# A hybrid encoder layer on one core: a tile of its own for half of the second projection tile's weights, other early orders, two projection blocks more ahead of the first scores, and a scaled copy moved into mask columns

## The chip, the cores and the metric

The kernel runs on one core of a Trainium2 chip. A core has a matrix engine (PE, with its weight loads shown as PEld), a vector engine (DVE), a scalar engine (ACT), a general engine (POOL) and a sync engine (SP) that issues most transfers. Each takes its instructions in a fixed order and they meet at semaphores. The metric is device time of one execution in microseconds, from runs of the whole program; the median of three counts.

## The reference

One encoder layer on 1024 tokens of width 1024, in float32. An RMS norm feeds one projection into 2304 columns, which serve two token mixers side by side.

```python
hn = rmsnorm(h, norm_mix[l])
proj = jnp.einsum('bsd,de->bse', hn, w_in[l])
qa, ka, va, qb, kb, vb = jnp.split(proj, splits, axis=-1)
...
o_a = window_gqa_sink(qa, ka, va, sink[l])
o_b = neighbourhood_attention(...)
mix = jnp.concatenate([rmsnorm(o_a, norm_a[l]), rmsnorm(o_b, norm_b[l])], axis=-1)
h = h + jnp.einsum('bse,ed->bsd', mix, w_out[l])
hn = rmsnorm(h, norm_ffn[l])
h = h + conv_gated_mlp(hn, w_gate[l], w_up[l], conv_w[l], conv_b[l], w_down[l])
return rmsnorm(h, norm_final)
```

Group A is attention in a window of 128 tokens either side, with 8 query heads on 2 key heads, rotated first quarters of the heads, and a sink logit in each softmax. Group B has 8 heads on a 16 by 64 grid of tokens with windows of 8 by 16 and a bias by relative position. Then come the output projection, a gated MLP of width 2816 with a convolution of three taps on the gate, and a last norm.

## The kernel before, in words

**Layout.** Activations stand transposed, features on the 128 partitions and 1024 tokens along the free axis. Nearly every product is made of two-part numbers: a value is split into a high part (written by ACT, which rounds it) and a low part (the remainder, by DVE or POOL), and a product is three matmuls, high by high, low by high, high by low. One such triple on 128 by 512 is a *block* (lines 172 to 174, in the loop of `product` line 180). A projection tile of 128 output columns takes 16 blocks: 2 halves of the tokens by 8 tiles of the inner axis k.

**The head of the program.** The first two projection tiles run together while x arrives (lines 742 to 747): for each k the scaled x tile is split (`split_scaled`, lines 191 and 192, high part on ACT, low part on DVE), and PE makes four blocks, two token halves by two tiles, into the PSUM banks `pj` and `o`. The weights of k = 0 to 3 of both come into four tiles that are made at the start; those of k = 4 to 7 go through `load_w`, that is a transfer into `raw` (2 buffers, line 150), the high part on ACT into `whi` (3 buffers, line 156) and the low part into `wlo` (3 buffers, line 157). Tiles of one name rotate: with three buffers, the fourth tile waits until the first one's readers are done. Beside this ACT squares the x tiles (line 211) and DVE adds the squares (line 213), for the norm.

**The third projection tile** (`third`, lines 750 to 757, 16 blocks into the bank `s`) fills PE while the norm is made. One of its blocks comes first; then 8 transposes of the summed squares (line 784); five blocks; 8 transposes that spread the inverse root over the partitions (line 266, called at 791); then the ten left. Between the two sets of transposes DVE sums (lines 785, 786) and POOL raises to the power of minus a half (line 787). The result `rstd` scales every evacuation of a projection from PSUM (`evacuate`, line 272).

**From a projection to attention.** `rotate` (lines 288 to 294) sends 16 rows of each head away by transfers, turns them on DVE and brings them back; the queries are then split and stacked (`split_first` lines 313 and 314 for the first query tile, `split_pair` lines 301 to 306 for others, `split_first_k` and `split_k` for keys).

**Attention.** There are 48 units: 16 window units (8 query blocks for each of 2 key heads, 4 heads each) and 32 grid units (8 heads by 4 pairs of query blocks). A softmax step (`softmax`, lines 465 to 495) starts with a score on PE (line 439), takes bias and row minimum on DVE (line 469) into a buffer of the rotation `p` (6 buffers), the exponential on ACT (line 473), the reciprocal on DVE (line 474), and then goes one of several ways. On way T, POOL scales (line 477) and PE transposes (line 501), and ACT and DVE split the transposed tile (lines 504, 505). On way D and Q the high part is made on ACT (line 488); the low part on D is one DVE pass (line 490), and on Q two POOL passes: a scaled copy `y` (line 493), which takes another buffer of the same rotation `p`, and the difference (line 494). Then a transposing transfer on SP (line 495) brings the result to `turned`, from where PE multiplies with the values (lines 528 and 604), and ACT and DVE take the sums out of PSUM (lines 539 and 543, 618 and 620). All 64 grid softmaxes are on way Q or T, 48 of them on Q.

**What sets the order.** PE's order is the program's own: it is written down as it stands. Between the steps of attention a generator, `rest()`, hands out blocks of the remaining projections (tiles 3 to 17, then the part of the output projection that needs group A alone); `fill(n)` takes n of them. `FILL0` blocks run before the first score, and `RATES` says how many are spread over each stretch of 8 window units or 4 grid units. The other engines' order is made by a scheduler which places an instruction when its model finds it ready, by priority; `behind(names)` keeps an instruction after a marked one. The weights of a later tile are fetched and split by `load` (k = 0 to 3) and `load_rest` (k = 4 to 7) of `Project`.

The constants tile `cst` holds the identity, the window mask (`K_MA`, 384 columns), the grid mask (`K_MB`) and a column of scales. Once attention is over, small vectors of the MLP's scales are taken from the window mask's columns (`littles`, line 1015).

## Time and profile before

| what | value |
| --- | --- |
| median of three runs | 1028.16 us (1027.82 to 1031.29) |
| profiled execution, its own time | 1027.81 us |
| its span, first to last instruction | 1026.0 us |
| PE busy | 1009.7 us, 98% |
| DVE, ACT, POOL busy | 875.6, 676.3, 216.4 us |
| granted PE clock, mean | 0.997 |

Busy time is the union of an engine's instructions. The rows of the timeline give start, duration, engine, line, operation, output and inputs, shape and count, and in brackets the engine's idle time before the row with what ended it. Matmuls are pipelined, so a matmul row lasts longer than the distance to the next one's start; what a wait costs PE is read from starts.

### The profile page before, as it was taken

What the parts mean: (1) busy time and instruction counts of PE and PEld (TensorE: products, weight loads), DVE (VectorE), ACT (ScalarE), POOL (GpSimd) and SP (SyncE); (2) the same over time, 40 slices, a digit from 0 to 9 for tenths busy, and PEclk for the clock granted to TensorE, in tenths of its full rate; (3) what the DMA queues carried; (4) which work ended last, traced back from release to release, by engine and by line L of the source; (5) the groups of instructions that cost most, each with busy time, mean ns of one, the idle gap of its engine ahead of it and who ended that gap; (6) DMA issues with size and microseconds to landing.
All of it is one profiled execution on the core that took longest, in us unless ns stands there. A gap on an engine that the chain in (4) does not pass through costs nothing.

```text
span 1026.0 us, 15565 instructions
## 1 busy us (share of the span) xinstructions
PE 1009.7 (98%) x5102; PEld 577.8 (56%) x5102; DVE 875.6 (85%) x1714; ACT 676.3 (66%) x1242; POOL 216.4 (21%) x339
## 2 busy tenths in 40 slices
PE   9999999999999999999999999999999999999997
PEld 7877777777775545544444444444444444444446
DVE  6799988767898899999897988788888888999875
ACT  8667787768687687645777777754634666655551
POOL 2235455877866210001000000000000000000002
PEclk9999999999999999999999999999999999999998
DMA  8556564787799875201787767633232788978744
GB/s 314 198 133 139 115 138 106 159 155 137 136 195 216 280 255 171 82 1 42 251 279 251 266 230 256 232 114 134 82 114 103 256 263 291 309 245 269 250 147 165
DMA packets 143938, 191.79 MB, mean 187 GB/s; under 512 B 77360, under 2 KB 88112, under 8 KB 143856
## 3 DMA queue, kind: packets, MB, share of 16 engines
q1 hardware_dynamic: 133264, 164.84, 55.9%
q10 hardware_dynamic: 10592, 25.95, 6.6%
q8 instruction: 40, 0.66, 0.3%
q14 instruction: 42, 0.34, 0.1%
HBM read 132.81 MB, written 28.57 MB: 157 GB/s over the span
## 4 chain that ended last, share of the span: by engine, by line
PE 65%; DVE 2%; DMA 1%; ACT 1%; issue 0%; POOL 0%; DVEq 0%; ACTq 0%; POOLq 0%
PE dn L1199 6%; PE dn L1200 6%; PE dn L1201 6%; PE pj L180 6%; PE z L1200 5%; PE z L1201 5%; PE z L1199 5%; PE y L1200 4%; PE y L1201 4%; PE y L1199 4%; PE x L1199 4%; PE x L1200 4%; PE x L1201 4%; PE ss L1239 1%; DMA turned<-stage 1%; DVE wlo L1174 0%
## 5 line engine op out<-in xcount | busy, mean ns | idle before, releaser
L1201 PEld LDWEIGHTS <-wlo 128*128 128x128 f16 x898 | 87.8, 98 | 101.2
L1199 PEld LDWEIGHTS <-whi 128*128 128x128 f16 x898 | 88.0, 98 | 100.3
L1200 PEld LDWEIGHTS <-whi 128*128 128x128 f16 x898 | 87.8, 98 | 100.3
L1201 PE MATMUL dn<-xd,wlo 128*128 128x512 f16 (+1 forms) x330 | 120.5, 365 | 0.0
L1200 PE MATMUL dn<-xd,whi 128*128 128x512 f16 (+1 forms) x330 | 120.5, 365 | 0.0
L1199 PE MATMUL dn<-xd,whi 128*128 128x512 f16 (+1 forms) x330 | 120.5, 365 | 0.0
L172 PE MATMUL pj<-xgh,whi 128*128 128x512 f32 x248 | 106.9, 431 | 0.0
L1201 PE MATMUL z<-hg,wlo 128*128 128x512 f16 x264 | 100.2, 379 | 0.0
L1199 PE MATMUL z<-hg,whi 128*128 128x512 f16 x264 | 100.2, 379 | 0.0
L1200 PE MATMUL z<-hg,whi 128*128 128x512 f16 x264 | 100.2, 379 | 0.0
L174 PE MATMUL pj<-xgh,wlo 128*128 128x512 f32 x248 | 97.7, 394 | 0.0
L173 PE MATMUL pj<-xgl,whi 128*128 128x512 f32 x248 | 97.6, 393 | 0.0
L473 ACT ACTIVATE p<-p,nm 128x385 f32<-128x385 f32 (+3 forms) x128 | 74.7, 584 | 34.6 <-DVE nm L469 28.6
L1173 ACT ACTIVATE whi<-ws,m 128x512 f16<-128x512 f32 (+1 forms) x96 | 65.8, 708 | 37.7 <-DVE ws L1340 22.9
L1174 DVE SCALAR_TENSOR_TENSOR wlo<-ws,m,whi 128x512 f16<-128x512 f32 (+1 forms) x96 | 70.3, 742 | 18.3 <-ACT whi L1173 18.1
L1054 POOL TENSOR_TENSOR back<-back,cst 128x4 f32<-128x4 f32 (+1 forms) x7 | 2.8, 395 | 356.8 <-DVE back L1053 356.8
L1188 ACT ACTIVATE scan<-scan 128x1024 f32<-128x1024 f32 (+1 forms) x60 | 61.1, 1018 | 18.4 <-DMA scan<-in_w_down_dram 13.2
L1173 ACT ACTIVATE whi<-raw,m 128x512 f16<-128x512 f32 (+1 forms) x78 | 51.1, 699 | 16.8 <-DMA raw<-in_w_down_dram 10.1
L1174 DVE SCALAR_TENSOR_TENSOR wlo<-raw,m,whi 128x512 f16<-128x512 f32 (+1 forms) x78 | 55.5, 733 | 6.7 <-ACT whi L1173 6.6
L1201 PE MATMUL y<-hg,wlo 128*128 128x512 f16 x160 | 60.7, 379 | 0.0
L1200 PE MATMUL y<-hg,whi 128*128 128x512 f16 x160 | 60.7, 379 | 0.0
L1199 PE MATMUL y<-hg,whi 128*128 128x512 f16 x160 | 60.7, 379 | 0.0
(296 smaller groups left out, 2464.7 us busy)
## 6 DMA issues: line engine op xcount, KB each, us to landing
xd<-x SPq DMA_DIRECT2D x77, 256.0 KB, 5.3
raw<-in_w_down_dram SPq DMA_DIRECT2D x64, 256.0 KB, 3.3
x<-c ACTq DMA_DIRECT2D x22, 512.0 KB, 4.2
scan<-in_w_gate_dram SPq DMA_DIRECT2D x18, 512.0 KB, 4.7
scan<-in_w_up_dram SPq DMA_DIRECT2D x18, 512.0 KB, 5.5
raw<-in_w_gate_dram SPq DMA_DIRECT2D x18, 512.0 KB, 3.5
raw<-in_w_up_dram SPq DMA_DIRECT2D x18, 512.0 KB, 3.6
raw<-in_w_in_dram SPq DMA_DIRECT2D x32, 256.0 KB, 3.2
```

Of the source, the lines that this page charges most:

```text
L172: nc.tensor.matmul(ps, w[0], x[0][:, tsl(h)], start=first, stop=False)
L173: nc.tensor.matmul(ps, w[0], x[1][:, tsl(h)], start=False, stop=False)
L174: nc.tensor.matmul(ps, w[1], x[0][:, tsl(h)], start=False, stop=last)
L180: nc.tensor.matmul(ps, a, b, start=i == 0 and b is x[h][0] and a is w[0], stop=i == len(ws) - 1 and a is w[1])
L473: nc.scalar.activation(p[:, 0:e], p[:, 0:e], AF.Exp, bias=nm, scale=-1.0, accum_out=sm)
L1173: mark["whi"] = nc.scalar.activation(hi, src, AF.Copy, scale=by)
L1174: nc.vector.scalar_tensor_tensor(lo, src, by, hi, op0=ALU.mult, op1=ALU.subtract)
L1188: nc.scalar.activation(t, t, AF.Square, accum_out=dst)
L1199: nc.tensor.matmul(ps, w[0], x[0], start=first and i == 0, stop=False, skip_group_check=True)
L1200: nc.tensor.matmul(ps, w[0], x[1], start=False, stop=False, skip_group_check=True)
L1201: nc.tensor.matmul(ps, w[1], x[0], start=False, stop=last and i == len(ws) - 1, skip_group_check=True)
L1239: nc.tensor.matmul(narrow[h][:, c:c + 1], s2[:, c * 128:(c + 1) * 128], ones[:, 0:1], start=c == 0 and d == ADDED[h] - 1, stop=d == KT - 1 ...
```

## The change

- The low and high parts of the second tile's weights for k = 4 to 7 go to a tile of their own, `wrest`, in the buffers named `mix`, and no longer take a buffer each of `whi` and `wlo`.
- The third tile has three blocks before the first transposes (one before), then five, then eight (ten before).
- `FILL0` is 24 (22 before), and the third and fourth of `RATES` are 21 (22 before).
- `load_rest` of the fifth tile (`jobs[2]`) is called from inside `split_first`, between the two halves of the first query tile, and the second half's low part is placed behind it. `load` of the tile after (`jobs[3]`) is called after the ninth step of the fifth, no longer at its start.
- The adds of squares are placed behind the low part of the x tile two further on.
- On way Q the scaled copy goes to the columns of the window mask, and no longer to a buffer of `p`. The small vectors get 15 columns of their own at the end of `cst` (`K_LITTLE`), so `cst` and its transfer have 912 columns (897 before). A small reduction of the MLP's gains is placed behind the first grid minimum.

The number of PE, DVE, ACT and POOL operations and their shapes are the same.

```diff
-FILL0, FILL1 = 22, 12
-RATES = [45, 49, 22, 22, 22, 22, 20, 18, 16, 14]
+FILL0, FILL1 = 24, 12
+RATES = [45, 49, 21, 21, 22, 22, 20, 18, 16, 14]
...
-K_ID, K_MA, K_MB, K_SCALE, K_END = 0, 128, 512, 896, 897
+K_ID, K_MA, K_MB, K_SCALE, K_LITTLE, K_END = 0, 128, 512, 896, 897, 912
...
-        def halve_w(raw):
+        def halve_w(raw, to=None):
-            hi, lo = (wpool.tile([128, 4, 128], F32R, name=n, tag=n) for n in ("whi", "wlo"))
+            hi, lo = to or (wpool.tile([128, 4, 128], F32R, name=n, tag=n) for n in ("whi", "wlo"))
...
-                        nc.vector.tensor_tensor(s2[:, cols], s2[:, cols], acc[:, cols], op=ALU.add)
+                        with behind(*[n for n in ("x low %d" % (k + 2),) if n in mark and k < 5]):
+                            nc.vector.tensor_tensor(s2[:, cols], s2[:, cols], acc[:, cols], op=ALU.add)
...
                 mark["stack"] = nc.scalar.activation(x[hi], t[hi], AF.Copy, scale=-HD ** -0.5)
-                mark["low"] = nc.vector.scalar_tensor_tensor(x[lo], t[hi], -HD ** -0.5, f32(x[hi, :]), op0=ALU.mult, op1=ALU.subtract)
+                mark.setdefault("stack a", mark["stack"])
+                with behind(*["weights low"] * (x is b)):
+                    mark["low"] = nc.vector.scalar_tensor_tensor(x[lo], t[hi], -HD ** -0.5, f32(x[hi, :]), op0=ALU.mult, op1=ALU.subtract)
+                if x is a:
+                    with behind("stack a"):
+                        between.pop()()
...
-                            y = apart(apool.tile([128, 384], F32, name="y", tag="p", bufs=PS, padded_shape=[128, 386])[:, 0:n])
+                            y = apart(cst[:, K_MA:K_MA + 128 * c])
...
-        for p in first:
-            p.w += load_w(w_in[p.m, :, 4:8, :])
+        first[0].w += load_w(w_in[first[0].m, :, 4:8, :])
+        rest = big("wrest", "mix", F32R)[:, :].rearrange("p (s k c) -> p s k c", s=2, c=128)
+        first[1].w += halve_w(fetch_w(w_in[first[1].m, :, 4:8, :]), (rest[:, 0], rest[:, 1]))
...
-        next(rest3)
+        for _ in range(3):
+            next(rest3)
...
-                if i + 2 < len(jobs):
-                    with behind(*["stack"] * (i == 1)):
-                        jobs[i + 2].load()
+                if i + 2 < len(jobs) and i != 1:
+                    jobs[i + 2].load()
...
                         if n == 8:
+                            between.append(jobs[2].load_rest)
...
+                    if i == 1 and n == 8:
+                        jobs[i + 2].load()
...
-                    with behind("stack", "copied"):
-                        with tc.high_priority(offset=500):
-                            jobs[2].load_rest()
...
-        littles = [K_MA, None]
+        littles = [K_LITTLE, None]
...
-            nc.vector.tensor_reduce(v, g, axis=mybir.AxisListType.X, op=ALU.max, apply_absolute_value=True)
+            with behind("grid"):
+                nc.vector.tensor_reduce(v, g, axis=mybir.AxisListType.X, op=ALU.max, apply_absolute_value=True)
```

On ACT, in the stretch where x arrives, the order was as follows: L191 is the high part of an x tile, from the fourth (k = 3) on, L156 the high part of weights, L211 a square.

```order
L191 ACTIVATE xgh<-xt,par 128x1024
L156 ACTIVATE whi<-raw 128x512
L191 ACTIVATE xgh<-xt,par 128x1024
L211 ACTIVATE sq<-xt 128x1024
L191 ACTIVATE xgh<-xt,par 128x1024
L211 ACTIVATE sq<-xt 128x1024
L191 ACTIVATE xgh<-xt,par 128x1024
L156 ACTIVATE whi<-raw 128x512
```

The same stretch with the change.

```order
L191 ACTIVATE xgh<-xt,par 128x1024
L156 ACTIVATE whi<-raw 128x512
L156 ACTIVATE wrest<-raw 128x512
L191 ACTIVATE xgh<-xt,par 128x1024
L211 ACTIVATE sq<-xt 128x1024
L191 ACTIVATE xgh<-xt,par 128x1024
L211 ACTIVATE sq<-xt 128x1024
```

The second tile's weights moved up by three x tiles; on DVE their low part moved up likewise.

On DVE around the first scores the order was as follows, from the low parts of the keys (L321, L322) and of the first query tile (L314) to the first row minimum (L469). The first L157 here is `load_rest` of the fifth tile, the second `load` of the sixth.

```order
L321 TENSOR_TENSOR kb<-t,ka 64x1024
L322 TENSOR_TENSOR ka<-t,ka 64x1024
L314 SCALAR_TENSOR_TENSOR q<-t,q 64x1024 x2
L272 TENSOR_TENSOR t<-pj,rstd_370 128x512
L157 TENSOR_TENSOR wlo<-raw,whi 128x512
L303 SCALAR_TENSOR_TENSOR t<-t,q 128x1024
L157 TENSOR_TENSOR wlo<-raw,whi 128x512
L469 ISA p,nm<-s,cst,nsink 128x256
```

With the change (its own line numbers: L319 is the low part of the first query tile, L304 that of the second, L273 an evacuation, L477 the minimum).

```order
L329 TENSOR_TENSOR kb<-t,ka 64x1024
L330 TENSOR_TENSOR ka<-t,ka 64x1024
L319 SCALAR_TENSOR_TENSOR q<-t,q 64x1024
L157 TENSOR_TENSOR wlo<-raw,whi 128x512
L319 SCALAR_TENSOR_TENSOR q<-t,q 64x1024
L273 TENSOR_TENSOR t<-pj,rstd_369 128x512
L304 SCALAR_TENSOR_TENSOR t<-t,q 128x1024
L273 TENSOR_TENSOR t<-pj,rstd_369 128x512
L477 ISA p,nm<-s,cst,nsink 128x256
```

The weights of `load_rest` moved ahead of the second half of the queries, those of `load` behind the first minima, and an evacuation stands ahead of these.

Towards the end of the grid units the DVE's order around the add into `sqb` (L973) was as follows; L168 is a low part of output weights, L693 an evacuation of the output projection.

```order
L505 TENSOR_TENSOR turned<-pt,turned 128x3x128
L168 SCALAR_TENSOR_TENSOR wlo<-raw,wo_by,whi 128x512
L469 ISA p,nm<-s,xb 128x384
L469 ISA nm 128x1
L469 ISA p,nm<-s,xb 128x256
L469 ISA nm 128x1
L973 TENSOR_TENSOR sqb<-sqb,sq 128x1024
```

With the change (L515 is the split of a transposed tile, L477 the minimum, L985 the add, L703 the evacuation).

```order
L515 TENSOR_TENSOR turned<-pt,turned 128x3x128
L477 ISA p,nm<-s,xb 128x384
L477 ISA nm 128x1
L985 TENSOR_TENSOR sqb<-sqb,sq 128x1024
L703 SCALAR_TENSOR_TENSOR h_4192<-pj,wo_back,xr 128x512
L484 RECIPROCAL sm<-sm 128x1
L477 ISA p,nm<-s,xb 128x256
L477 ISA nm 128x1
L168 SCALAR_TENSOR_TENSOR wlo<-raw,wo_by,whi 128x512
```

The first of the two minima stands ahead of the weights' low part now, the second behind the add and an evacuation.

More of the change, by code (lines that the diff above doesn't have):

```diff
@@ L191, in split_scaled @@
             nc.scalar.activation(hi, src, AF.Copy, scale=scale)
-            nc.vector.scalar_tensor_tensor(lo, src, scale, f32(hi[:, :]), op0=ALU.mult, op1=ALU.subtract)
+            mark["split"] = nc.vector.scalar_tensor_tensor(lo, src, scale, f32(hi[:, :]), op0=ALU.mult, op1=ALU.subtract)
             return hi, lo
@@ L307, in split_pair @@
             return [a, b]
+        between = []
         def split_first(t):
@@ L468, in softmax @@
                         nc.gpsimd.tensor_copy(p[:, n:n + 1], nsink)
-                    nc.vector.tensor_tensor_reduce(
+                    minimum = nc.vector.tensor_tensor_reduce(
                         out=apart(p[:, 0:n]), in0=apart(ps[:, 0:n]), in1=bias, scale=1.0, scalar=3e38 if nsink is None else nsink,
                         op0=ALU.add, op1=ALU.min, accum_out=nm)
+                    if nsink is None:
+                        mark.setdefault("grid", minimum)
                     e = n if nsink is None else n + 1
@@ L744, in hybrid_layer @@
                 xg[k] = split_scaled(xts[k], col(C_NMIX + k), "xg", "xg")
+                mark["x low %d" % k] = mark["split"]
             for h in range(2):
```

## The prediction

> **What bounds the kernel now.** I read the page's busy shares first, then PE's waits in stretches, then starts on PE's timeline.
>
> ```profile
> PE 1009.7 (98%) x5102; PEld 577.8 (56%) x5102; DVE 875.6 (85%) x1714; ACT 676.3 (66%) x1242; POOL 216.4 (21%) x339
> ```
>
> PE is busy for all but 16.3 us of the span of 1026.0, and the change neither adds nor removes a matmul. So it can only fill gaps or make new ones. PE's waits, as the table of waits gives them for 0 to 38, 38 to 160 and 160 to 345 us (total, times, longest):
>
> ```profile
> PE o L172 <- ACT whi L156: 0.7, 1, 0.7
> PE o L174 <- DVE wlo L157: 0.2, 1, 0.2
> ...
> PE o L528 <- DVE mixa L543: 1.3, 2, 1.0
> PE o L528 <- DVE turned L505: 1.0, 1, 1.0
> ...
> PE o L604 <- DMA turned<-stage: 1.1, 2, 0.9
> PE o L604 <- DMA turned<-hl: 0.5, 1, 0.5
> PE pt L501 <- POOL p L477: 0.4, 1, 0.4
> ```
>
> The longest of each stretch are 0.9 us before the first scores, 2.3 us in the window units and 2.0 us late in the grid units. That is 5.2 us, 0.5% of the span, so a change that removed them all would just reach what a measurement can tell from none (about 0.5%, 5.1 us).
>
> **The change part by part.**
>
> *The second tile's weights.* PE stands at k = 4 of the second tile:
>
> ```profile
> 18.29 0.39 PE L173 MATMUL pj<-xgl,whi 128*128 128x512 f32 x1
> 18.51 0.39 PE L174 MATMUL pj<-xgh,wlo 128*128 128x512 f32 x1
> 19.61 0.50 PE L172 MATMUL o<-xgh,whi 128*128 128x512 f32 x1 [0.71 <-ACT whi L156]
> ...
> 20.91 0.40 PE L172 MATMUL pj<-xgh,whi 128*128 128x512 f32 x1
> ```
>
> Start to start is 0.22 to 0.23 us without a wait (18.29 to 18.51). The four steps from 18.51 to 20.91 took 2.40 us and would take 0.91, so this stall costs 1.49 us, more than the 0.9 of idle time in the table. The fourth tile named `whi` had to wait for readers of the first, which PE finishes at k = 3; ACT then made it at 18.94.
>
> ```profile
> 13.38 0.63 ACT L156 ACTIVATE whi<-raw 128x512 fp32r<-128x512 f32 x1
> 13.92 1.14 ACT L191 ACTIVATE xgh<-xt,par 128x1024 fp32r<-128x1024 f32 x1
> ...
> 18.94 0.61 ACT L156 ACTIVATE whi<-raw 128x512 fp32r<-128x512 f32 x1
> ...
> 8.61 0.81 SPq L150 DMA_DIRECT2D raw<-in_w_in_dram  x2
> ...
> DMA to landing us min/median/max: 5.3/5.3/5.3
> ```
>
> With `wrest` it stands right behind the first tile's part. Its transfer, the second of the pair that SP issues from 8.61 on (at about 9.1), lands 5.3 us later, at 14.4. ACT, free at about 13.9, waits 0.5 us there, ends `wrest` at 15.0 and the next x tile's high part at 16.1; DVE (0.6 us for the weights' low part, 1.2 for the x tile's) is done near 17.3. PE wants both at 18.1 to 18.7. So nothing late is left: **minus 1.49 us**. If the landing slips by more than the 0.8 us that are left, the excess comes off this.
>
> *Three blocks, five, eight.* Without this PE, 1.49 us early, would meet the transposes before their input:
>
> ```profile
> 29.41 1.22 DVE L213 TENSOR_TENSOR sq<-sq 128x1024 f32<-128x1024 f32 x1
> 31.84 0.69 DVE L157 TENSOR_TENSOR wlo<-raw,whi 128x512 fp32r<-128x512 f32 x1 [1.22 <-ACT whi L156]
> 32.45 1.28 DVE L785 TENSOR_REDUCE gains<-st 128x4 f32<-128x512 f32 x2
> 34.09 1.66 POOL L787 TENSOR_TENSOR gains<-gains,minus_half 128x8 f32<-128x8 f32 x1 [6.30 <-DVE gains L786]
> 35.22 0.39 PE L174 MATMUL s<-xgh,wlo 128*128 128x512 f32 x1
> 35.80 1.09 PE L266 MATMUL sw<-cst,gains 128*128 128x128 f32 x8 [0.19 <-POOL gains L787]
> ```
>
> The sum of squares ends at 30.6 (about 31.0 with ACT's 0.5 us lag). PE came to its transposes at 31.1; now at 31.1 - 1.49 + 2 x 0.68 = 31.0, so no wait appears (bounds: 0 to +0.5). The weights' low part at 31.84, which waited for ACT, no longer stands before the reduction, since ACT's order has it before the scans of output weights. The root is then ready at about 34.9 and PE wants it at 35.2. The step 35.22 to 35.80 shrinks from 0.58 to 0.23: **minus 0.35 us**.
>
> *The first scores.* PE is now 1.84 us early with two blocks (1.37 us) more ahead of the scores, so the first one starts at 58.52 - 1.84 + 1.37 = 58.05.
>
> ```profile
> 53.30 2.46 DVE L314 SCALAR_TENSOR_TENSOR q<-t,q 64x1024 fp32r<-64x1024 f32 x2
> 56.40 0.68 DVE L157 TENSOR_TENSOR wlo<-raw,whi 128x512 fp32r<-128x512 f32 x1
> ...
> 54.44 0.39 PE L172 MATMUL pj<-xgh,whi 128*128 128x512 f32 x1
> 58.52 0.28 PE L439 MATMUL s<-ka,q 128*128 128x256 f32 x1
> ```
>
> The fifth tile starts at 54.44; its fifth block's last matmul, at 57.62, uses the weights done at 57.08. Early by 1.84, PE would want them at 55.8. Moved between the two halves of the queries, they are done at 53.30 + 1.23 + 0.68 = 55.2, even if DVE's chain of turned heads gains nothing; the second half then ends at 56.4, 1.6 us before its first score. I take **zero** (bounds: 0 to +0.7). A split of the sixth tile's weights goes behind the minima and an evacuation before them, 0.6 us each: DVE's first minimum stays near 59.0.
>
> *The window units.* Two blocks are work done ahead and are kept whatever follows; the other 0.47 us of lead is not, wherever DVE sets the time. There it does so once:
>
> ```profile
> 75.10 1.21 DVE L345 TENSOR_TENSOR kb<-t,ka 64x1024 fp32r<-64x1024 f32 x1
> 76.24 0.68 DVE L272 TENSOR_TENSOR t<-pj,rstd 128x512 f32<-128x512 f32 x1
> 76.84 0.41 DVE L505 TENSOR_TENSOR turned<-pt,turned 128x256 f16<-128x256 f32 x1
> 77.30 0.27 PE L528 MATMUL o<-turned,v 128*128 128x256 f16 x1 [1.02 <-DVE turned L505]
> ```
>
> The split at 76.84 is the second of its kind. Now the evacuation (0.68 us) comes ahead of the first, but two passes of a later tile's turning, shorter each than the evacuation, ahead of both. Removing this wait gives -1.2; the lost lead and those passes give at most 0.47 + 2 x 0.68 = +1.8. Every later collision of such ops (the 1.3 us on L543) is dealt anew. Nothing favours a side: **zero**, bounds -2.6 to +2.5.
>
> *The grid units.* The scaled copy leaves the rotation `p`, so minima wait less for POOL.
>
> ```profile
> 318.46 0.92 POOL L494 TENSOR_TENSOR hl<-y,hl 128x384 f16<-128x384 f32 x1
> 319.03 0.90 DVE L168 SCALAR_TENSOR_TENSOR wlo<-raw,wo_by,whi 128x512 f16<-128x512 f32 x1
> 319.85 0.54 DVE L469 CUSTOM_DVE_ANT_0 p<-s,xb 128x384 f32<-128x384 f32 x1
> 322.71 0.58 POOL L477 TENSOR_SCALAR p<-p,sm 128x384 f32<-128x384 f32 x1 [3.33 <-DVE sm L474]
> ```
>
> The minimum at 319.85 stands behind weights (0.9 us) and after a POOL pass that ends at 319.4; POOL then idles 3.3 us for its reciprocal, and PE waits for POOL. One column set for 48 copies costs nothing, since POOL makes and uses each in turn. But only the first of two minima moves up; the second stands behind `sqb` and an evacuation. Of 2.0 us I take **minus 0.4** (bounds: -2.0 to +1). Two blocks fewer in units 16 to 23, where no wait of the table lies, cost zero.
>
> The transfer of 15 columns more and the small reduction are hidden: no PE wait stands near either.
>
> *Sum.* -1.49 - 0.35 - 0.40 = -2.24. The profiled execution took 1027.81 us, so 1025.6; the median of the runs shown is 0.35 higher, so **1025.9 us**.
>
> One rule bears on the fetches that start earlier, since `raw` is free at 15.7 and not 20.5. DMA is full then (the share is the last number but one, GB/s the last):
>
> ```profile
> 18.00:20.00 2.00, 1.29 (x6) 0.70 (x5) 2.00 (x3) 2.00 (x4) 0.00 (x0) 1.00 1.02 398
> ```
>
> Were transfers in flight to share evenly, about 1.2 MB more (weights and two scans) at 398 GB/s would hold the third tile's weights up by 3 us, and PE, which has about 1 us there, would give back 2: 1027.9 us. [...]
>
> **The rivals.**
>
> *A, the lead is given back* (1025.9 + 1.84 = 1027.7 us). PE comes early and waits for what it did not wait for: the first scores, or DVE at 77 us. For it: DVE, the third busy time of the row, fills 0.96 of 106 to 116 us.
>
> ```profile
> 106.00:116.00 10.00, 9.49 (x56) 6.65 (x55) 9.63 (x32) 7.34 (x20) 3.59 (x9) 1.00 0.73 167
> ```
>
> Against it: 1.37 of the 1.84 us are finished blocks. It needs 1.8 us of waits that the table does not have.
>
> *B, the waits of attention go too.* The 4.3 us after 38 us vanish, of which the sum has 0.4: 1025.9 - 3.9 = 1022.0 us. For it: the minima are freed. Against: only one order in three that I compared moved the right way.
>
> *C, slower.* In the window units DVE's in-order queue puts a 1.2 us op of a later tile ahead of the split that the running unit's product waits for, as at 75.10. Each collision costs about 1.2 us. Two more cancel the 2.2 us, from the third on the kernel is slower; with four, 1025.9 + 4.8 = 1030.7 us. For it: every row from 58 us on is re-dealt. Against: the 16 units had three such waits (those on L543 and L505), and the change adds no op.
>
> *D, the freed `p` buffers do nothing*, DVE's order being what holds a minimum: 1026.3 us, inside the forecast's own range.
>
> **How the numbers follow.** Forecast with D 0.56 (1024.4 to 1027.4), A 0.20, B 0.13, C 0.11. The range of 1022.8 to 1029.0 leaves out about a third of B and half of C. Faster than 1023.0 (0.5%) is just over half of B: 0.07. Slower than 1033.3 is C with six collisions or something unseen: 0.04. Within: 0.89.
>
> **What would show it.** Right: no wait of PE on `wrest` near 18.5; the transposes at 31.0 and 35.2 without a gap; the first score near 58.0; the sum of PE's waits before 60 us down by about 1. Wrong: a wait on x tiles or the third tile's weights between 18 and 31 us, a wait at the first scores, or waits on L515 or L553 (the old L505 and L543) above 3 us in total between 60 and 160 us.

## The result, and the profile after

The changed kernel took **1035.08 us** (median of 6 runs, 1033.42 to 1036.51) against 1028.29 us before (6 runs): a ratio of 1.0064, 95% interval 1.0054 to 1.0074. It is 6.6 us slower by the ratio; 1025.9 us was forecast, and the time lies 6 us above the range. Its profiled execution took 1034.38 us, with a span of 1032.6 us.

PE's busy time is nearly the same, 1009.7 us before and 1009.9 after, while its idle time grew from 16.3 to 22.7 us. So the time went into waits, and PE's table of waits for 38 to 160 and 160 to 345 us (total, times, longest) names them:

```profile
PE pt L511 <- DVE turned L515: 2.5, 1, 2.5
PE o L538 <- DVE mixa L553: 1.3, 2, 0.9
...
PE o L614 <- DMA turned<-hl: 6.6, 3, 2.9
PE o L614 <- DVE turned L515: 0.6, 1, 0.6
```

On PE's timeline (start, duration, in brackets the idle time before and what ended it), the head and the four long waits:

```profile
18.35 0.39 PE L174 MATMUL pj<-xgh,wlo 128*128 128x512 f32 x1
18.58 0.39 PE L172 MATMUL o<-xgh,wrest 128*128 128x512 f32 x1
...
19.03 0.39 PE L174 MATMUL o<-xgh,wrest 128*128 128x512 f32 x1
...
30.82 1.03 PE L797 MATMUL st<-cst,sq 128*128 128x128 f32 x8
35.12 1.04 PE L267 MATMUL sw<-cst,gains 128*128 128x128 f32 x8
...
57.78 0.28 PE L447 MATMUL s<-ka,q 128*128 128x256 f32 x1
...
76.43 0.52 PE L511 MATMUL pt<-cst,p 128*128 128x128 f32 x3 [2.47 <-DVE turned L515]
...
192.74 0.38 PE L614 MATMUL o<-turned,v 128*128 128x256 f16 x2 [2.87 <-DMA turned<-hl]
...
310.55 0.38 PE L614 MATMUL o<-turned,v 128*128 128x256 f16 x2 [1.08 <-DMA turned<-hl]
320.37 0.38 PE L614 MATMUL o<-turned,v 128*128 128x256 f16 x2 [2.62 <-DMA turned<-hl]
```

The head did as forecast: `wrest` is used at 18.58 without a wait, both sets of transposes start unhindered, the first score comes at 57.78. After that PE meets one wait of 2.5 us in the window units, one of 2.9 us in the first grid units and two late in the grid. The longest wait of before in these stretches was 1.0 us.

One count differs from what stands ahead of the prediction: DVE has 1715 operations (1714 before) and POOL 338 (339 before). The low part of one tile of weights is now made on DVE; experiment 3 comes back to it.

From PE's starts I made a table of *lost time*: for every matmul the distance to the next start less what its shape takes without a wait by these starts (0.228 us for 128x512 float32 and 0.2156 for 128x512 float16, where the commonest distances in the kernel before are 0.227 and 0.216 us, and so on), summed by stretch. It is the comparison used below (us; each from one profiled execution).

| kernel | 0–38 | 38–60 | 60–165 | 165–200 | 200–300 | 300–350 | rest |
| --- | --- | --- | --- | --- | --- | --- | --- |
| before | 5.9 | -0.1 | 5.8 | 0.8 | 3.3 | 3.5 | 3.6 |
| the change | 3.8 | -0.1 | 7.1 | 4.2 | 3.2 | 7.0 | 4.2 |
| difference | -2.1 | 0.0 | +1.3 | +3.4 | -0.1 | +3.5 | +0.6 |

The differences add to 6.6 us, the difference of the spans. A single execution can lie 1 to 2 us off the median of its kernel.

**The clock.** One part of this is no wait. After the wait that ends at 320.37 the granted clock (the third number from the end) drops to half. On PE's timeline two 128x512 float16 matmuls then start 0.42 to 0.45 us apart, where they start 0.216 us apart at full clock:

```profile
320.00:321.00 1.00, 0.63 (x4) 0.42 (x5) 0.00 (x0) 0.66 (x2) 0.36 (x1) 1.00 0.86 283
321.00:322.00 1.00, 1.00 (x5) 0.58 (x4) 0.00 (x0) 1.00 (x1) 0.91 (x1) 0.68 1.11 247
322.00:323.00 1.00, 1.00 (x4) 0.48 (x2) 0.88 (x3) 0.28 (x1) 0.01 (x1) 0.50 1.23 246
323.00:324.00 1.00, 1.00 (x5) 0.56 (x4) 0.82 (x1) 0.42 (x2) 0.00 (x0) 0.50 1.21 388
324.00:325.00 1.00, 1.00 (x5) 0.44 (x4) 0.01 (x1) 0.39 (x1) 0.00 (x0) 0.61 2.47 254
325.00:326.00 1.00, 1.00 (x9) 0.69 (x6) 1.00 (x3) 0.34 (x1) 0.09 (x1) 1.00 0.16 35
```

The shares below 1 add up to 0.32 + 0.50 + 0.50 + 0.39 = 1.7 us lost on top of the wait.

### The profile page after: what moved, and what is told of

Same layout as the page of the kernel before. It is cut to its first block, busy times and chain, and to the rows that moved or that the text cites. A ratio compares the mean times of both kernels' runs of the same rounds, so it can differ in the third digit from the quotient of the medians.

```text
span 1032.6 us, 15630 instructions
## 1 busy us (share of the span) xinstructions
PE 1009.9 (98%) x5102; PEld 577.4 (56%) x5102; DVE 877.3 (85%) x1715; ACT 677.1 (66%) x1242; POOL 216.4 (21%) x338
## 4 chain that ended last, share of the span: by engine, by line
PE 76%; DVE 3%; DMA 1%; issue 1%; POOL 0%; ACT 0%; DVEq 0%; ACTq 0%; POOLq 0%
PE pj L180 7%; PE dn L1213 6%; PE dn L1214 6%; PE dn L1212 6%; PE z L1213 5%; PE z L1214 5%; PE z L1212 5%; PE y L1214 4%; PE y L1213 4%; PE y L1212 4%; PE x L1212 4%; PE x L1214 4%; PE x L1213 4%; PE pj L172 2%; PE pj L174 2%; PE pj L173 2%
## 5 line engine op out<-in xcount | busy, mean ns | idle before, releaser
L1186 ACT ACTIVATE whi<-ws,m 128x512 f16<-128x512 f32 (+1 forms) x96 | 65.9, 708 | 36.5 <-DVE ws L1353 22.7
```

The lines of the kernel that those rows point to most:

```text
L1186: mark["whi"] = nc.scalar.activation(hi, src, AF.Copy, scale=by)
```

## The experiments

All ratios are against runs of the kernel before on the same chip. I began with what the trace suggests first, that the copy in one place had made POOL's passes late (behind `L572` and `L573` in the first grid units), and that this made the waits on `turned<-hl`.

**1. Parts alone, and parts undone.** *The head alone* has the edits of `halve_w`, `wrest`, the three blocks and the squares, and is otherwise the kernel before.

```diff
+        first[1].w += halve_w(fetch_w(w_in[first[1].m, :, 4:8, :]), (rest[:, 0], rest[:, 1]))
...
-        next(rest3)
+        for _ in range(3):
+            next(rest3)
```

> The kernel before with the changes of its first 36 us alone: the own tile for the second tile's weights, three, five and eight blocks, and the squares behind the x tiles. From the third projection tile on every engine has the order of before. Theory 'head is right': the stalls of 1.49 and 0.35 us are gone and the lead is kept, 1028.3 - 1.84 = 1026.4 us. Rival 'the lead is given back' at the wait of 1.2 us near 76 us and in later waits on DVE: 1027.5 to 1028.3 us.

Measured: 1029.08 us, ratio 1.0009 (1.0000 to 1.0018). The two stalls are gone, but the lead is given back before the first score. The rows of DVE and PE near the fifth tile's weights:

```profile
53.80 2.46 DVE L315 SCALAR_TENSOR_TENSOR q<-t,q 64x1024 fp32r<-64x1024 f32 x2
56.30 0.69 DVE L273 TENSOR_TENSOR t<-pj,rstd 128x512 f32<-128x512 f32 x1
56.90 0.68 DVE L157 TENSOR_TENSOR wlo<-raw,whi 128x512 fp32r<-128x512 f32 x1
```

```profile
57.64 0.50 PE L174 MATMUL pj<-xgh,wlo 128*128 128x512 f32 x1 [1.30 <-DVE wlo L157]
```

PE, early, waits 1.3 us for a weight split that stands behind both halves of the queries. That is the wait which the moved `load_rest` of the change takes away.

*The copy alone*, in the kernel before:

```diff
-y = apart(apool.tile([128, 384], F32, name="y", tag="p", ...)[:, 0:n])
+y = apart(cst[:, K_MA:K_MA + 128 * c])
```

> The kernel before with one part alone: the scaled copy of way Q goes to the mask columns, and the small vectors to their own 15 columns. Theory 'copy': it is what put PE's waits on the transposing transfers of the low parts (turned from hl) into the grid units; by PE's lost time in the changed kernel against before (+3.0 us at 185 to 200, +4.5 at 300 to 325, -1.1 at 325 to 350) it costs 6.4 us: 1034.7 us. Rival 'the two blocks fewer' or 'the moved weights re-deal the order': nothing happens here, 1028.3 us; the prediction's own value for this part was -0.4, 1027.9 us.

Measured: 1027.29 us, ratio 0.9989 (0.9980 to 0.9998): faster by 1.1 us. My theory of the copy fell here.

*The change with the copy back in `p`*, the same edit the other way:

> The changed kernel with one part undone: the scaled copy is back in a buffer of the rotation p. Theory 'copy': 1035.1 - 6.4 = 1028.7 us, and the waits at 189 us and 309 to 320 us are gone while the one near 73.6 us (2.6 us) stays. Rivals 'two blocks fewer' and 'moved weights': 1035.1 us or 0.4 us more.

Measured: 1035.32 us, 1.0067 (1.0053 to 1.0080). The theory fell from this side too: the lost time at 300 to 350 us is 7.0 us as in the change. One piece of it holds in the trace: POOL again makes the source of that transfer ahead of the bias tiles, and PE's wait near 192 us is 1.8 us and not 2.9. But the time of the kernel is no shorter.

*The change with the weights of the fifth and sixth tiles where they were* (`rest()` and `split_first` of the kernel before):

```diff
-                    with behind("stack a"):
-                        between.pop()()
...
+                    with behind("stack", "copied"):
+                        with tc.high_priority(offset=500):
+                            jobs[2].load_rest()
```

> The changed kernel with one part undone: the later half of the fifth tile's weights and the early half of the sixth's are fetched and split where the kernel before had them. Theory 'moved weights re-deal the window units': the wait of 2.6 us near 73.6 us goes, a wait of about 1 us as before may stand in its place, 1032.5 to 1033.5 us; the grid waits stay if 'copy' holds. If the moved weights made the grid waits too: 1027 to 1029 us. If the two added blocks ahead of the first scores made the wait at 73.6 us: 1035.1 us.

Measured: 1033.81 us, 1.0051 (1.0038 to 1.0063). The wait at 73 us goes, the one on `wlo` near 56 us comes back (1.2 us), and the grid keeps its waits: 4.7 us lost at 165 to 200 us, 6.7 at 300 to 350. So the moved weights are needed for the window wait and have no part in the grid's. They don't make the 2.5 us by themselves: with them and 22 blocks ahead (*Undone in the change*, below) PE waits 0.9 and 0.8 us there.

**2. The blocks.** What is left is `FILL0` and `RATES`.

```diff
-FILL0, FILL1 = 22, 12
-RATES = [45, 49, 22, 22, 22, 22, 20, 18, 16, 14]
+FILL0, FILL1 = 24, 12
+RATES = [45, 49, 21, 21, 22, 22, 20, 18, 16, 14]
```

*This alone*, in the kernel before:

> The kernel before with one part alone: 24 blocks ahead of the first score and 21 in place of 22 in each of the two stretches of units 16 to 23. The prediction's value for this part is zero, 1028.3 us. Theory 'blocks': this part, with the new order that it makes the scheduler deal to the other engines, made the waits near 189 us and at 300 to 325 us (PE's lost time there is 3.0 and 4.5 us above before): 1034 to 1035 us. Rival 'only together': no part does it alone, 1028 to 1029 us.

Measured: 1033.09 us, 1.0049 (1.0037 to 1.0061). *Undone in the change*, all else as changed:

> The changed kernel with one part undone: 22 blocks ahead of the first score, 22 and 22 in units 16 to 23, all else as changed. Theory 'blocks': the waits at 73, 189 and 300 to 325 us go, the head's lead of 1.84 us is kept because the fifth tile's weights come early (the wait of 1.5 us at 56 us, which the head alone met, is gone), and the copy adds its 1.1 us: 1028.3 - 1.8 - 1.1 = 1025.4 us. Rival 'only together' or 'moved weights re-deal': 1033 to 1035 us.

Measured: 1026.92 us, 0.9988 (0.9979 to 0.9997). So two numbers of a table cost 5.0 us alone and, by the two ratios (1.0064 and 0.9988), 7.8 us in the change. Without them the change is a little faster than the kernel before.

*Two blocks ahead, taken from the first window units* (`FILL0` 24, `RATES` 43, 49, 22, 22), and *two blocks moved from units 16 to 23 into the first window units* (`FILL0` 22, `RATES` 47, 49, 21, 21):

> The kernel before with 24 blocks ahead of the first score, taken from the first eight window units (43 in place of 45), the grid units keeping their 22 and 22. If the two blocks that the grid units lost are what counts: 1028 to 1029 us and no wait above 1 us near 189 us. If two blocks ahead of the first score are what counts: 1033 to 1035 us, as with the blocks taken from the grid. If any new count re-deals the order by chance: a time apart from both.

> The kernel before with 22 blocks ahead of the first score as it was, and two blocks moved from units 16 to 23 (21 and 21) into the first eight window units (47). If the two blocks that the grid units lost are what counts: waits of 3 us or more in units 16 to 23 and late in the grid, 1033 to 1035 us. If the two ahead of the first score are what counts: 1028 to 1029 us.

Measured: 1031.89 us, 1.0032 (1.0020 to 1.0045), and 1030.46 us, 1.0022 (1.0011 to 1.0033). Both cost, and neither as forecast. From here on a kernel is named by its numbers: 24; 21, 21 means `FILL0` 24 and 21, 21 as the third and fourth of `RATES`, and a further pair in front of these is the first and second. I counted the blocks that PE has done before a score, in the written order of each kernel (score steps: 4 to a window unit, 2 to a grid unit).

| blocks before score step | 0 | 68 | 72 | 76 | 80 | 84 | 100 |
| --- | --- | --- | --- | --- | --- | --- | --- |
| before (22; 22, 22) | 38 | 142 | 151 | 162 | 173 | 184 | 228 |
| the change (24; 21, 21) | 40 | 144 | 151 | 161 | 172 | 182 | 226 |
| 24; 22, 22 | 40 | 144 | 151 | 162 | 173 | 184 | 228 |
| 22; 21, 21 | 38 | 142 | 151 | 161 | 172 | 182 | 226 |

In all four 151 blocks stand ahead of step 72: the kernel before takes 9 between steps 68 and 72, and with two done ahead it takes 7. So the two early blocks are swallowed there, and 21 and 21 then take away two that nothing gives back: from step 84 on the changed kernel is two blocks short. The table suggests two separate edits.

The reason for the 151 that the next expectation gives, a tile that must be finished, was wrong, as the generator's own answers show when the program is built. What swallows the blocks is a refusal:

```python
while len(waiting) > 2:
    settle(0)
    if len(waiting) > 2:
        yield False
...
def fill(n):
    while n > 0 and next(filler, False):
        n -= 1
```

With more than two finished tiles waiting for operand buffers the generator answers False, `fill` stops, and the blocks asked for are not asked for again. In window unit 15 the kernel before has three refused, with 24 ahead it is five, with 43 in the first window units four, with 47 five. So 24; 43, 49, 22, 22 is one block short from step 72 on, and 47, 49, 21, 21 two.

*The change with 24; 22, 22*, *24 alone* and *21, 21 alone* (both in the kernel before), and for the direction *23, 23 alone*:

> The changed kernel with 24 blocks ahead of the first score, but 22 and 22 in units 16 to 23 as before. Counted on PE's order, the block count then equals that of the kernel before from the 72nd score step on (151, 173, 195 blocks at steps 72, 80, 88), while the changed kernel stands two short (151, 172, 193): before the first grid score the generator is made to finish a tile anyway, and the two early blocks only replace two of those. Theory 'two short': the waits in the grid units go, 1035.1 - 3.0 (185 to 200 us) - 3.5 (300 to 350 us) = 1028.6 us or a little less with the gain of the copy. Rival 'the early blocks re-deal the order': 1033 to 1035 us, since they are still there.

> The kernel before with 24 blocks ahead of the first score and nothing else; from the 72nd score step on PE's order is that of before. Theory 'two short': 1028.3 us, no wait above 1.5 us in the grid units. Rival 'the early blocks re-deal the order': 1031 to 1034 us, as with the blocks moved (1033.1).

> The kernel before with 21 and 21 in units 16 to 23 and nothing ahead: PE's order is that of before until the 72nd score step, and two blocks short of it from the 84th on. Theory 'two short': the waits near 189 us and at 300 to 325 us come, and the splits of the mixed outputs (mg), which wait for the last projection block to free its buffers, begin near 293 us and not at 288: 1032 to 1035 us. Rival 'the early blocks': 1028.3 us.

> The kernel before with 23 and 23 in units 16 to 23: two blocks more than before from the 84th score step on. If being short is what costs, and the grid units of before are still short of blocks late (transfers there are issued 3.2 to 6 us before their use): the splits begin near 284 us and the late waits shrink, 1025 to 1028 us. If any other count than 22 and 22 costs because the order of the other engines is dealt anew: 1030 to 1034 us.

Measured, with the lost time of the two stretches that matter:

| kernel | us | ratio (95%) | 165–200 | 300–350 |
| --- | --- | --- | --- | --- |
| the change | 1035.08 | 1.0064 (1.0054 to 1.0074) | 4.2 | 7.0 |
| the change, 24; 22, 22 | 1031.53 | 1.0038 (1.0024 to 1.0051) | 4.2 | 2.2 |
| the change, 22; 22, 22 | 1026.92 | 0.9988 (0.9979 to 0.9997) | 1.5 | 2.4 |
| 24; 21, 21 alone | 1033.09 | 1.0049 (1.0037 to 1.0061) | 5.5 | 5.9 |
| 24 alone | 1029.65 | 1.0017 (1.0008 to 1.0026) | 5.5 | 4.0 |
| 21, 21 alone | 1033.52 | 1.0047 (1.0034 to 1.0059) | 0.9 | 6.0 |
| 23, 23 alone | 1035.53 | 1.0070 (1.0057 to 1.0082) | 1.4 | 9.9 |
| 24; 43, 49, 22, 22 alone | 1031.89 | 1.0032 (1.0020 to 1.0045) | 0.8 | 5.6 |
| 22; 47, 49, 21, 21 alone | 1030.46 | 1.0022 (1.0011 to 1.0033) | 2.9 | 2.9 |
| before | | 1 | 0.8 | 3.5 |

Up to 23, 23 the table seems to separate by the two numbers: with 24 ahead 4 us or more are lost at 165 to 200 us, with 22 only 0.8 to 1.5; with 21, 21 some 6 to 7 us at 300 to 350 us, with 22, 22 only 2.2 to 4.0. The two kernels moved from and into the window break both rules: 24; 43, 49, 22, 22 loses 0.8 and 5.6 us, 22; 47, 49, 21, 21 loses 2.9 and 2.9. For the first stretch the count of blocks fits all of them: every kernel of the table with 7 blocks between score steps 68 and 72 loses 2.9 us or more there, and those with 8 (43 in the window), 9 or 10 (23, 23) lose 0.8 to 1.5. For the second stretch no count fits all. The kernels with 184 blocks ahead of step 84, as before, lose 2.2 to 4.0 us (the head and the moved weights without the rest, experiment 5, 4.7), those with 182, 183 or 186 lose 5.6 to 9.9, but 22; 47, 49, 21, 21, with 182, loses 2.9 (and 4.6 at 200 to 300 us). "Short" was the wrong word in any case: two blocks *more* cost most of all. Alone, any count other than that of before was slower, by 1.7 to 7.2 us.

In the change the two numbers part as follows, by the ratios of 0.9988, 1.0038 and 1.0064: the two early blocks cost 5.1 us and 21, 21 on top of them 2.7 us. In the kernel before, 24 alone costs 1.7 us and 21, 21 alone 4.8. Two profiled executions are poor witnesses of their kernels' times: that of the change with 24; 22, 22 was the fastest of its five, 2.3 us below the median, and that of 24 alone the slowest of its eleven, 1.5 us above.

**3. Why the first grid units wait.** In the kernel before, the transposing transfer that PE needs at 190.06 is issued at 185.96:

```profile
190.06 0.39 PE L604 MATMUL o<-turned,v 128*128 128x256 f16 x2
```

```profile
185.96 1.29 SPq L495 DMA_TRANSPOSE turned<-hl  x1
```

That is 4.1 us. Between 160 and 345 us of the kernel before such transfers landed 2.4 to 5.7 us after their issue, the median 3.3. By the median this place, which has no wait, had some 0.8 us to spare, an estimate. In most other grid units of before the distance is 6.5 to 11.6 us up to 280 us, and 3.2 to 6.1 us from 300 us on. What PE has to do while such a transfer is under way is its *cover*. The early blocks take two blocks of cover, 1.37 us, from between steps 68 and 72. In the change the transfer is also late, issued at 189.34, since POOL makes its source after the bias tiles:

```profile
185.43 0.58 POOL L503 TENSOR_SCALAR cst<-p,sm 128x384 f32<-128x384 f32 x1
185.99 0.58 POOL L487 TENSOR_SCALAR p<-p,sm 128x384 f32<-128x384 f32 x1
186.54 0.99 POOL L572 TENSOR_TENSOR xb<-cst,rr 128x384 f32<-128x384 f32 x1
187.50 0.71 POOL L573 TENSOR_TENSOR xb<-cst,rr 128x256 f32<-128x256 f32 x1
188.17 0.91 POOL L504 TENSOR_TENSOR hl<-cst,hl 128x384 f16<-128x384 f32 x1
189.34 1.24 SPq L505 DMA_TRANSPOSE turned<-hl  x1
```

With 24 alone POOL makes that source ahead of the bias tiles, as before, and the transfer is issued at 187.0, 1.0 us later than before, about as much as PE itself is late (0.9 us at step 68). PE still waits 2.0 us:

```profile
186.96 1.23 SPq L495 DMA_TRANSPOSE turned<-hl  x1
...
191.69 0.56 PE L604 MATMUL o<-turned,v 128*128 128x256 f16 x2 [1.99 <-DMA turned<-hl]
```

PE was ready at 189.70, 2.74 us after the issue, where before it had 4.10: the lost 1.36 us are the two blocks. But the transfer took 4.7 us here and at most 4.1 before. So 1.4 us of the wait go with the cover and 0.6 us with a longer flight (the time from issue to use), of which no run shows the cause. There the clock falls too, to 0.50 from 192 to 194 us, so this place loses 3.9 us.

One thing comes along with the two blocks in every kernel that has them ahead at this point: the low part of one tile of weights is made on DVE near 163 us, and POOL's next one stands ahead of that source (at 183.15 us with 24 alone) and not behind it (185.09 before). Cover and this order were not taken apart.

**4. Why the late grid units wait.** SP's issues near 300 us, of the kernel before and of 21, 21 alone; `xr` is a tile of x for the output projection, 512 KB:

```profile
295.93 0.58 SPq L682 DMA_DIRECT2D xr<-in_xT_dram  x1
298.17 1.26 SPq L495 DMA_TRANSPOSE turned<-stage  x1
299.48 0.58 SPq L682 DMA_DIRECT2D xr<-in_xT_dram  x1
301.28 1.21 SPq L495 DMA_TRANSPOSE turned<-stage  x1
```

```profile
298.12 1.24 SPq L495 DMA_TRANSPOSE turned<-stage  x1
299.42 1.04 SPq L682 DMA_DIRECT2D xr<-in_xT_dram  x2
301.04 1.29 SPq L495 DMA_TRANSPOSE turned<-stage  x1
```

With 21, 21 both x loads stand ahead of one transposing transfer, and PE waits for it:

```profile
307.08 0.27 PE L604 MATMUL o<-turned,v 128*128 128x128 f16 x2 [2.40 <-DMA turned<-stage]
```

Its flight is 307.08 - 301.04 = 6.0 us. With 23, 23 it is the same, worse:

```profile
299.82 1.05 SPq L682 DMA_DIRECT2D xr<-in_xT_dram  x2
301.17 1.51 SPq L495 DMA_TRANSPOSE turned<-stage  x1
```

```profile
308.93 0.58 PE L604 MATMUL o<-turned,v 128*128 128x256 f16 x2 [5.38 <-DMA turned<-stage]
```

7.8 us in flight, and then the granted clock is at 0.5 from 308 to 314 us. To tell the x loads from the order of the engines, the second x load was placed behind those transposing transfers, in both of these, in the change and in the kernel before. PE's and POOL's orders are the same as without the edit, but those of ACT and DVE change from about 300 us on, so the loads are not the only thing that differs.

```diff
-                    nc.sync.dma_start(xt, xT[d])
+                    with behind(*["flip"] * (d == 1)):
+                        nc.sync.dma_start(xt, xT[d])
```

> The kernel with 21 and 21 alone (1033.5 us), and the second of the two x loads placed behind the transposing transfers that it stood ahead of. PE's and POOL's orders are the same. Theory 'x loads': the transfer issued near 301 us flies 3.3 to 4.4 us and not 6.0, PE's wait of 2.4 us near 304 us goes and those on POOL and the stage transfer behind it (1.2 and 1.5 us) shrink: 1030 to 1031.5 us. Rival 'the order of POOL, ACT and DVE' or 'two blocks less cover': 1033.5 us.

> The kernel with 23 and 23 alone (1035.5 us), with the same move of the second x load. Theory 'x loads': the transfer that flew 7.8 us lands in 3.3 to 4.4, PE's wait of 5.4 us near 303 us falls by 3.5 us or more: 1030 to 1032 us. Rival: 1035.5 us.

> The changed kernel (1035.1 us) with the same move of the second x load. Here the loads stood apart, each ahead of one transposing transfer (issued 301.4 and 304.5 us), and PE waited 1.1 us at 309 and 2.6 us at 317 us. Theory 'x loads': the first of these goes, the second, which begins with a transposing transfer whose issue alone took 3.1 us, may stay: 1032 to 1034 us. Rival: 1035 us.

> The kernel before with the same move of the second x load, which stood ahead of a transposing transfer that PE did not wait for. Theory 'x loads': nothing to gain but 0.3 us (the wait of 0.2 us near 302 us), 1027.5 to 1028.5 us. If the later x load makes the sums that need it late: 1029 to 1031 us.

Measured: 1033.29 us (1.0040, 1.0027 to 1.0054), 1034.33 (1.0053, 1.0040 to 1.0065), 1037.34 (1.0083, 1.0068 to 1.0097) and 1031.17 (1.0026, 1.0017 to 1.0035). In time the forecast of this theory failed; in the trace its first half held. SP and PE of the kernel with 21, 21 and the later load:

```profile
299.09 0.57 SPq L683 DMA_DIRECT2D xr<-in_xT_dram  x1
300.71 1.22 SPq L495 DMA_TRANSPOSE turned<-stage  x1
```

```profile
304.62 0.27 PE L604 MATMUL o<-turned,v 128*128 128x128 f16 x2 [0.28 <-DMA turned<-stage]
...
321.15 1.01 PE L180 MATMUL pj<-mg,whi 128*128 128x512 f16 x2 [3.21 <-DVE h L694]
```

The flight falls from 6.0 to 3.9 us and the wait from 2.4 to 0.3. But the tile that now comes later is needed by an evacuation (`h`, L694), and PE waits 3.2 us for that at 321 us. The kernel before gets the same new wait (2.9 us). With 23, 23 one x load less ahead takes the flight from 7.8 to 6.4 us only:

```profile
299.23 0.58 SPq L683 DMA_DIRECT2D xr<-in_xT_dram  x1
300.57 1.26 SPq L495 DMA_TRANSPOSE turned<-stage  x1
```

```profile
306.92 0.59 PE L604 MATMUL o<-turned,v 128*128 128x256 f16 x2 [3.94 <-DMA turned<-stage]
```

So both pairs, one execution each, say that the second x load lengthened the flight, by 2.1 and 1.4 us; the 6.4 us behind a single load say that it is not all. In the change itself the long wait is another one, at 317 us. POOL had the source of its transfer ready at 313.80, SP issued it at 315.99, behind two transfers of turned rows (in the kernel before one of the two stands behind it), and its flight was 4.4 us; no run tests this. That the load can be put anywhere better was not shown.

**5. What the rest is worth.** The change without its blocks and without its copy, and once more the change without its blocks, on one chip:

> The changed kernel without its blocks (22 ahead, 22 and 22) and without its copy (back in a buffer of p): the head and the moved weights remain. If the head's lead of 1.84 us survives once the fifth tile's weights come early: 1026.5 us. If the lead is lost to DVE in the window units, as the trace of the rest shows (first score 1.9 us early, the 16th step on time), and the gain is the copy's: 1028.0 to 1028.7 us.

> The changed kernel without its blocks, once more: head, moved weights and copy. It should repeat 1026.9 us, about 0.15 per cent below the kernel before; the difference to the run above is the copy's share on this chip (1.1 us by the copy alone).

Measured: 1029.45 us (1.0014, 1.0006 to 1.0023) and 1027.32 us (0.9992, 0.9983 to 1.0001). Head and moved weights together don't gain: they cost 1.5 us (0.6 to 2.3), more than either value expected. The copy is worth 1.1 us alone and 2.1 us here. Of the 2.1 us, 0.3 lie outside the span: in all 11 runs without the copy time less span is 2.0 to 2.2 us, with it 1.7 to 1.9. The best versions, the rest of the change and the copy alone, are 0.1% faster than the kernel before, less than the 0.5% that was set as a difference.

## Why the prediction was wrong, step by step

- **The second tile's weights, -1.49, and three, five, eight blocks, -0.35: right at their place, not in the time of the kernel.** In profiled executions the first 38 us lose 3.8 to 4.8 us (mean 4.1 of 9) with the new head and 5.4 to 5.9 (mean 5.6 of 11) without: 1.5 us, of the 1.84 forecast. The head's start varies by up to 1 us from execution to execution. The sum left out the 2 us that evenly shared transfers would have cost, on an assumption that no run shows; they did not come, for PE waits nowhere for x tiles or the third tile's weights between 18 and 31 us. But the sum carried the 1.84 us to the end of the kernel, and no run shows that: the head alone is 0.9 us slower than before (0 to 1.9), with the moved weights 1.5 us.
- **The first scores, zero: right**, the first is at 57.78 us and 58.05 was forecast. The price of the edit if left out, which the working did not give, is the 1.3 us that the head alone waits at 57.6.
- **The window units, zero with bounds -2.6 to +2.5: inside, at +1.3.** The collision was named with its place: an evacuation (0.7 us) and passes of a later tile ahead of the split on which PE waits. It came at 73 us, in the trace with both the moved weights and the early blocks:

```profile
73.94 1.28 DVE L387 SCALAR_TENSOR_TENSOR vhl<-t,down,vhl 64x1024 f16<-64x1024 f32 x1 [0.30 <-ACT vhl L386]
75.26 0.69 DVE L273 TENSOR_TENSOR t<-pj,rstd 128x512 f32<-128x512 f32 x1
75.87 0.41 DVE L515 TENSOR_TENSOR turned<-pt,turned 128x256 f16<-128x256 f32 x1
```

  It cost 2.5 us; the wait of 1.0 us at 154 us went. Waits on L515 and L553 come to 4.0 us between 38 and 160 us, so the sign that the prediction named for being wrong here, more than 3 us, did show.
- **"Two blocks are work done ahead and are kept whatever follows": the first step that failed.** They were kept until window unit 15, where two more requests are refused for want of operand buffers. The count of blocks ahead of each score, read from the order, shows it before any run. What the sum had at zero cost 5.1 us in the change (by 1.0038 against 0.9988).
- **"Two blocks fewer in units 16 to 23, where no wait of the table lies, cost zero": the second step that failed.** Two mistakes stand in it. The change was read as moving two blocks, where with the refusals it takes two away from the rest of attention. And the absence of a wait was taken for slack: at 190 us there was some 0.8 us by the median flight of 3.3, late in the grid 0 to 3. This step cost 2.7 us on top of the early blocks in the change and 4.8 us alone; both steps together measured +7.8 us where the sum has nothing.
- **The copy, -0.4 with bounds -2.0 to +1: right in sign**, -1.1 (interval -2.1 to -0.2). The profiled execution doesn't show where; its own time is 1.8 us above its median.
- **Rival A** (the lead is given back, 1027.7) is what the rest of the change does. Its 1026.9 and 1027.3 us are below that by the copy; without the copy it is at 1029.45, so the lead is more than given back. PE is 1.9 us early at the first score, on time (+0.03 and -0.35) at the 12th step. **Rival C** had the kind of thing, a new order in which the ops that PE needs stand behind others, but looked for it in the window units, priced a collision at 1.2 us and did not look at DMA. **Rival B** did not come about in any run. **Rival D** holds in the changed kernel (1035.3 us with the copy back in `p`), not without its blocks.
- **The range** had no term for a wait that changes the clock (below).

Not settled: why one or two blocks more or fewer at step 84 turn the order of DVE, ACT and SP near 300 us into a worse one in all but one of the kernels tried. The order is the scheduler's, and PE's written order there differs only by these blocks.

## What to carry to other kernels

Where PE's order is written out and other engines are ordered by a scheduler, a number that shifts two blocks is a change to every unit behind it: count the blocks ahead of each score in both orders before pricing it, and ask whether a request can be refused. No wait is not slack: measure the distance from issue to use of what PE needs, and price a shift where that distance is nearest to the shortest flight. Price a wait for the clock too: after some waits of 2.0 us and more the granted clock was 0.5 here, and in the change that cost 1.7 us on top of the wait (next section).

## What the runs showed of the hardware

- **After some waits of 2 us and more the granted clock was 0.5.** It fell to 0.5 after waits of 2.0 us (24 alone, near 191 us, and 24; 21, 21 alone), 2.1 (two blocks from the window, 304 us), 2.5 (the change with the copy back in `p`, 76 us) and 2.6 (the change, 320 us), three times in the change with the later x load (PE idle 2.5 us from 70 to 80, 2.95 from 190 to 195 and 3.1 from 320 to 330 us), and after all four waits of 3.2 us or more: 0.50 in stretches of 1 or 2 us of 24 alone, 23, 23 alone and the change, 0.54 to 0.82 as means of 5 us. In the change that lost 1.7 us more, by the shares of the clock from 321 to 325 us, and in both kernels with 23, 23 it lost 3.4 us, by those from 305 to 315 us. After others of 2.4 to 2.9 us (among them 21, 21 alone at 307 us, the change at 76 and 193 us) it stayed at 1.00.
- **The length of the wait alone does not tell which.** In the change PE waits 2.47 us ahead of 76.43 and the clock is 1.00 from 75 to 80 us; with the copy back in `p` PE is idle for 2.48 us from 70 to 80 us, and the clock is 0.67 from 75 to 80. In 24; 21, 21 alone the wait of 2.0 us near 191 us is followed by 0.76 from 190 to 195 us, and the one of 1.98 us ahead of 309.56 by 1.00 from 310 to 315. No run tested what sets the two kinds apart.
- **Flights of transposing transfers.** Between 160 and 345 us they landed 2.4 to 5.7 us after their issue in the kernel before, the median 3.3, and 2.4 to 5.3 us in the change, the median 3.1. From issue to a use that waited it was 3.4 us in the change near 189 us, 3.9 and 6.4 us behind one load of 512 KB, 6.0 and 7.8 us behind two, and 4.7 us in two kernels with no such load right ahead (24 alone, and 24; 21, 21 alone, near 187 us).
